# A matvec on VectorE: turning its result rows into columns through DRAM instead of on TensorE

## The chip, the cores and the metric

The kernel runs on one core of a Trainium2 chip. The metric is the device time of one execution in microseconds, from the start to the end of the program on that core. The kernel before was timed three times; the median is 1687.03 us (1686.95 to 1689.38). A separate execution was taken with the hardware profiler: it took 1689.57 us, and its span, from the first to the last instruction in the trace, is 1687.9 us.

The engines appear under short names: PE is TensorE (PEld its weight loads), DVE is VectorE, ACT is ScalarE, POOL is GpSimd, SP is SyncE, which in this kernel only issues transfers.

## The reference

One layer of a transformer-like backbone with token mixing and an MLP, for 128 context tokens and 256 latent tokens (384 in all), width 2048. Each of the two groups of tokens has a condition vector (c_ctx and c). From it the layer computes six modulation vectors of 2048 values:

```python
def _adaln(cond, ada_w, ada_b):
    mod = jax.nn.silu(cond) @ ada_w + ada_b          # (2048) @ (2048, 6*2048)
    return mod.reshape(cond.shape[0], N_MOD, D_MODEL)

# in the layer:
shift_a, scale_a, gate_a, shift_f, scale_f, gate_f = ...   # mod[:, 0..5]
h = _rmsnorm(x, norm_w[0]) * (1 + scale_a) + shift_a
...                                                  # projections, mLSTM heads, pooling
mix = jnp.concatenate([hm, hp], axis=-1) @ w_out
x = x + gate_a * _rmsnorm(mix, norm_w[1])
h = _rmsnorm(x, norm_w[2]) * (1 + scale_f) + shift_f
y = jnp.square(jax.nn.relu(h @ w1)) @ w2             # hidden width 8192
x = x + gate_f * _rmsnorm(y, norm_w[3])
```

Everything is float32. The change touches only how shift_f, scale_f and gate_f are brought into the layout in which they are used. What is computed stays the same.

## The kernel before

**Layout.** Activations are kept transposed: a tile holds 128 features (one per partition) by 384 tokens. A modulation value belongs to a feature, so it is needed as a column: one value per partition. The tile `mod` (line 212) is 128 x 6 x 16 x 2: for each of the six vectors (index i; 1 is scale_a, 2 gate_a, 3 shift_f, 4 scale_f, 5 gate_f), each of the 16 blocks of 128 features, and each of the two groups of tokens, one value per partition.

**Large products.** Each float32 product is made of three faster matmuls: both operands are split into a high and a low part. A weight piece of 512 KB is loaded by SP (`load_w`, line 122), ACT makes the high part (line 134), DVE the low part (line 135), and PE does high x high, high x low, low x high (lines 143 to 145). Three raw pieces and four high and low pieces (N_W) may be in flight. The order of the stages is: input projection (lines 481 to 520), then q and k with attention and pooling beside them, the output gate o, the output projection `w_out` (line 896; 32 pieces, for eight groups of 256 columns: four each, the first two groups in turns), then the MLP: w1 and w2. For chunks 1 to 7 of the MLP the w2 product is made in seven block products instead of eight (`mlp_seven`, lines 1192 to 1270; its matmuls are lines 1222 to 1224, its splits lines 1208 and 1209).

**The modulation vectors.** Some of them are computed on PE (`ada_mat`, `ada_gate`, `ada_eight`). The rest are made by `ada_vec(i, c, n)` (line 292) on DVE, as a generator which the large products advance step by step (`Feed`, line 150). It does a matvec for n columns of `ada_w` and both groups of tokens:

- The rows of `ada_w` are loaded in slabs, t = 0, 1, ... (line 300). For each slab and each group of tokens DVE multiplies by one value per partition and adds to the accumulator `ada_acc` (lines 314 and 316). With n = 1024 or in the later calls with n = 512 there are 16 slabs of one row per partition, two DVE operations each.
- Line 329: eight matmul records with a block of ones sum over the partitions. The sums appear in PSUM as rows: four rows (on partitions 0, 32, 64, 96), for two halves of the columns and two groups of tokens.
- Line 331: ACT copies them to `adav_sb` in SBUF. Then the generator yields.
- Line 335: matmuls with `adav_sb` as weights and four columns of the identity turn the rows into columns, in a fresh PSUM bank `adaf`: four matmuls for n = 1024, two for n = 512.
- `ada_finish` (line 277), once per half: DVE adds the bias (line 280) and, for scales and gates, multiplies by a norm weight (lines 285 and 288), and writes `mod`.

It is called eight times. `mid_vec` (line 786) makes five calls with n = 1024 beside q, k, o and `w_out`: i = 4 twice, i = 3 twice, then i = 2 once. In each, `mat` (line 816), a part of gate_a made on PE, advances at some steps. `gate_f` (line 966) makes three calls with n = 512 for i = 5 beside the MLP, the last two at a quarter of a step per product (RATE_GS); after the last call PE transposes the whole of gate_f to rows (line 976, `gfT`), which POOL writes to DRAM (`gf_dram`, line 978) for use at the end of the kernel (line 1132).

**Order.** In the first part PE, DVE and ACT follow the written order, then, up to line 520, PE alone. In most of the rest a planner orders the instructions of each engine when the program is built: it takes the instructions whose inputs it expects to be ready, those written earlier first. Each engine then works through its list strictly in order, and an instruction that waits holds up those behind it. Transfers issued by POOL stand in POOL's list, between its own operations: the power of line 200 for the norms of attention, the masks of line 682, and loads and stores of states.

Of the kernel before, what the change touches and what calls it, by code (L numbers as in the profile page):

```python
# [7 lines left out]
F32 = mybir.dt.float32  # L8
# [5 lines left out]
P = 128  # L14
# [29 lines left out]
def hymba_kernel(  # L44
# [6 lines left out]
    nc = tc.nc  # L51
    w_in, w_out, w1, w2, ada_w = w_in[0], w_out[0], w1[0], w2[0], ada_w[0]

    const = ctx.enter_context(tc.tile_pool(name="const", bufs=1))
# [5 lines left out]
    dram = ctx.enter_context(tc.tile_pool(name="dram", bufs=1, space=bass.MemoryType.DRAM))  # L60

    def slot(name, dt=F32):
        return slots.tile([P, 386], dt, tag="t", name=name)

    def bank(name):
        return psum.tile([P, 512], F32, tag="ps", name=name)
# [172 lines left out]
    def ada_mat(parts, tags=("ada",), raws=None):  # L239


        n, nk = len(parts), parts[0][2]
        w, nj = nk * P, 8 // nk
        ps = bank(f"ada_{parts[0][0]}_{parts[0][1]}")
        for b, (i, k0, _) in enumerate(parts):
            c0 = i * D + k0 * P
            for j0 in range(0, 16, nj):
                tag = tags[b % len(tags)]
                raw = raws.pop(0) if raws else None
                if raw is None:  # L250
                    raw = (wp if tag == "lo" else adap).tile([P, nj, w], F32, tag=tag, name=f"ada_raw_{i}_{k0}_{j0}", bufs=N_W if tag == "lo" else N_ADA)
                    nc.sync.dma_start(raw, aw[:, j0:j0 + nj, c0:c0 + w])
                for a in range(nj):
                    j = j0 + a
                    g = j % 4
                    nc.tensor.matmul(ps[32 * g:32 * g + 32, 0:w], cT[:, j, 6 - 2 * b:38 - 2 * b], raw[:, a, :],
                                     start=b == 0 and j < 4, stop=b == n - 1 and j >= 12)
                if b < n - 1 or j0 + nj < 16:
                    yield
        yield from ada_rows(parts, ps)  # L260
# [16 lines left out]
    def ada_finish(i, k0, nk, ps):  # L277

        v = mod[:, i, k0:k0 + nk, :]
        nc.vector.tensor_tensor(  # L280
            v, ps,
            abias[:, i, k0:k0 + nk].unsqueeze(2).to_broadcast([P, nk, 2]), op=ALU.add)
        if i in (1, 4):
            w = nw[:, i // 2, k0:k0 + nk].unsqueeze(2).to_broadcast([P, nk, 2])
            nc.vector.scalar_tensor_tensor(v, v, 1.0, w, op0=ALU.add, op1=ALU.mult)
        elif i in (2, 5):
            w = nw[:, 1 if i == 2 else 3, k0:k0 + nk].unsqueeze(2).to_broadcast([P, nk, 2])
            nc.vector.tensor_tensor(v, v, w, op=ALU.mult)

    vec = {}  # L290

    def ada_vec(i, c, n):


        acc = vec["acc"].tile([P, 2, n], F32, tag="adaacc", name=f"ada_acc_{i}_{c}", bufs=1)
        c0, nj = i * D + c, vec["slab"] // n

        def load(t):
            raw = vec["pool"].tile([P, nj, n], F32, tag="ada", name=f"ada_raw_{i}_{c}_{t}", bufs=vec["bufs"])
            nc.sync.dma_start(raw, aw[:, nj * t:nj * t + nj, c0:c0 + n])  # L300
            return raw

        beside = vec.get("beside", {})
        raw = load(0)
        yield
        for t in range(16 // nj):
            if t in beside:
                next(beside[t], None)
            ahead = load(t + 1) if t < 16 // nj - 1 else None
            for a in range(nj):  # L310
                for g in range(2):
                    cj = sg[:, g, nj * t + a:nj * t + a + 1]
                    if t == 0 and a == 0:
                        nc.vector.tensor_scalar(acc[:, g, :], raw[:, a, :], cj, None, op0=ALU.mult)
                    else:
                        nc.vector.scalar_tensor_tensor(acc[:, g, :], raw[:, a, :], cj, acc[:, g, :], op0=ALU.mult, op1=ALU.add)  # L316
            raw = ahead
            if ahead is not None:
                yield
        yield  # L320
        w = n // 2
        nk = w // P
        if "end" in beside:
            next(beside["end"], None)
        ps = bank(f"adav_{i}_{c}")
        for h in range(2):
            for g in range(2):
                r = 32 * (2 * h + g)
                nc.tensor.matmul(ps[r:r + 32, 0:w], ones[:, 0:32], acc[:, g, h * w:(h + 1) * w], start=True, stop=True)
        sb = vec["pool"].tile([P, 512], F32, tag="adasb", name=f"adav_sb_{i}_{c}", bufs=1)  # L330
        nc.scalar.activation(sb[:, 0:w], ps[:, 0:w], AF.Copy)
        yield
        pf = bank(f"adaf_{i}_{c}")
        for k in range(nk):
            nc.tensor.matmul(pf[:, 4 * k:4 + 4 * k], sb[:, k * P:(k + 1) * P], ident[:, 0:P:32], start=True, stop=True)
        for h in range(2):
            ada_finish(i, c // P + nk * h, nk, pf[:, 0:4 * nk].rearrange("p (k r) -> p k r", r=4)[:, :, 2 * h:2 * h + 2])
        yield
# [87 lines left out]
    h = []  # L426
# [25 lines left out]
    def load_chunk(s, ci, after=(), later=None):  # L452
        kind, c0, w = chunks[ci]
        ks = slice(ksteps[s][0], sum(ksteps[s]))
        if kind == "u":
            n, pieces = w, [(0, wv_in[:, ks, U0 + c0:U0 + c0 + w])]
        else:
            n, pieces = w * P, [(0, wv_in[:, ks, V0 + c0 * P:V0 + (c0 + w) * P])]
            if c0 == 6:
                pieces.append((n, wv_in[:, ks, 4 * M:4 * M + 32]))  # L460
                n += 32
        return load_w(pieces, f"{kind}_{c0}_{s}", ksteps[s][1] * n, after, later) + (n,)
# [18 lines left out]
    for s in range(NS):  # L481
        for ci, (kind, c0, w) in enumerate(chunks):
            k0, nk = ksteps[s]
            hi, lo, n = w_first if s == 0 and ci < 2 else load_chunk(s, ci, h_ins if s == 0 else ())
# [301 lines left out]
    def mid_vec():  # L786
        for i, q in ((4, 0), (4, 1), (3, 0), (3, 1), (2, 0)):
            yield from ada_vec(i, 1024 * q, 1024)
# [100 lines left out]
    for cols in ([0, 256], [512], [768], [1024], [1280], [1536], [1792]):  # L889
        if cols[0] in (768, 1024, 1280):  # L890
            for m in range(2):
                n = len(early)
                t = y[n // 2][:, 1024 * (n % 2):1024 * (n % 2) + 1024].rearrange("p (j c) -> p j c", c=256)
# [72 lines left out]
    def gate_f():  # L966
        yield from ada_mat([(5, 0, 2), (5, 2, 2)], raws=early)
        for q in (1, 2, 3):
            yield from ada_vec(5, 512 * q, 512)
            if q == 1:  # L970
                vec["half"] = True
                while vec["half"]:
                    yield
        ps = bank("gfT")
        t = slot("gfT")[0:32, 0:P]
        nc.tensor.transpose(ps[0:32, 0:P], mod[:, 5].rearrange("p k g -> p (k g)"), ident)
        nc.vector.tensor_copy(t, ps[0:32, 0:P])
        nc.gpsimd.dma_start(gf_dram, t)
        yield
# [3 lines left out]
    for k in range(KT):  # L983
        xr.append(slot(f"xTr{k}"))
        nc.gpsimd.dma_start(xr[k][:, 0:NTOK], xT_dram[:, k, :])
    gfg = gate_f()

    def fill():
# [400 lines left out]
```

## Time and profile before

| | |
|---|---|
| time, median of 3 runs | 1687.03 us |
| time of the profiled execution | 1689.57 us |
| its span, first to last instruction | 1687.9 us |
| PE busy | 1656.9 us (98%) |
| DVE busy | 1340.3 us (79%) |
| ACT busy | 752.4 us (45%) |
| POOL busy | 130.9 us (8%) |
| bytes moved, mean rate | 320.95 MB, 190 GB/s |
| mean granted clock of PE | 0.997 |

The profile is one execution, seen by the hardware profiler. A row of the timeline has the start and the duration in microseconds, the engine, the line, the operation, the tile written and the tiles read, the shapes and a count; in brackets stand the idle time of the engine just before, and what ended it. The table of windows gives for each stretch its length and the busy time of each engine with the number of instructions, then PE's granted clock (1.00 is full), the mean busy share of the 16 DMA engines and what they moved in GB/s. The chain of waits is followed back from the last instruction: its rows are start, duration, engine, tile and line. Matmuls are pipelined, so their durations overlap: what one costs is read from the starts of its neighbours.

### The profile page before, as it was taken

To read this page: it belongs to the slowest core of one execution; us is meant where nothing else is said; L and a number is where in the kernel's file an instruction comes from. 1 tells how busy PE (TensorE), PEld (TensorE's weight loads), DVE (VectorE), ACT (ScalarE), POOL (GpSimd) and SP (SyncE) were. 2 spreads that over 40 slices of the span, in tenths; PEclk is the share of its full clock that TensorE was granted. 3 is DMA by queue.
4 is the path that set the end of the run, shared out by engine and by line. 5 is a ranking of instruction groups with operands and counts; after the bars stand their busy time and mean duration, and the time that the engine had idled before them with its cause. 6 is when DMAs were issued, how large, how long until landed. Compare 5 with 4: busy or idle time off the path is not lost.

```text
span 1687.9 us, 27859 instructions
## 1 busy us (share of the span) xinstructions
PE 1656.9 (98%) x10965; PEld 1582.5 (94%) x10965; DVE 1340.3 (79%) x2009; ACT 752.4 (45%) x1225; POOL 130.9 (8%) x181
## 2 busy tenths in 40 slices
PE   6999999999999999999999999999999999999997
PEld 4888999999999989989999999999999999999996
DVE  3677769898999959997797688988588488588688
ACT  4332355555443345543444444444444444444443
POOL 0000002221000024430000000000000000000120
PEclk9999999999999999999999999999999999999999
DMA  9999857777789964754546245544344443433653
GB/s 319 316 296 298 277 160 256 238 250 223 237 270 309 311 203 129 217 153 126 173 152 194 88 138 173 158 150 140 110 150 127 124 138 114 149 122 112 187 183 134
DMA packets 258195, 320.95 MB, mean 190 GB/s; under 512 B 14752, under 2 KB 223248, under 8 KB 257680
## 3 DMA queue, kind: packets, MB, share of 16 engines
q1 hardware_dynamic: 250256, 303.41, 57.0%
q0 software_dynamic: 5856, 13.69, 2.8%
q10 hardware_dynamic: 1952, 2.07, 0.4%
q8 instruction: 86, 1.41, 0.3%
q14 instruction: 45, 0.37, 0.1%
HBM read 308.61 MB, written 10.51 MB: 189 GB/s over the span
## 4 chain that ended last, share of the span: by engine, by line
PE 90%; DVE 4%; DMA 3%; issue 1%; SPq 1%; ACT 0%; POOL 0%; DVEq 0%; ACTq 0%; POOLq 0%
PE acc_w L144 10%; PE acc_w L143 10%; PE acc_w L145 10%; PE y L1223 4%; PE y L1224 4%; PE y L1222 4%; PE v L495 4%; PE u L495 3%; PE acc_wo L143 3%; PE acc_wo L144 3%; PE acc_wo L145 3%; PE y_yz L1223 2%; PE y_yz L1222 2%; PE y_yz L1224 2%; PE y L1066 2%; PE y L1065 2%
## 5 line engine op out<-in xcount | busy, mean ns | idle before, releaser
L144 PE MATMUL acc_w<-h2l,hi_w 128*128 128x384 f32 (+1 forms) x1024 | 346.2, 338 | 0.5 <-DVE h2l L1016 0.5
L143 PE MATMUL acc_w<-h2h,hi_w 128*128 128x384 f32 (+1 forms) x1024 | 344.2, 338 | 1.2 <-ACT h2h L1012 1.2
L145 PE MATMUL acc_w<-h2h,lo_w 128*128 128x384 f32 (+1 forms) x1024 | 345.1, 337 | 0.0
L135 DVE TENSOR_TENSOR lo_w<-raw_w,hi_w 128x1024 fp32r<-128x1024 f32 x152 | 185.3, 1221 | 137.0 <-ACT hi_w L134 136.8
L134 ACT ACTIVATE hi_w<-raw_w 128x1024 fp32r<-128x1024 f32 x152 | 160.8, 1058 | 215.2 <-PE acc_w L144 94.9
L316 DVE SCALAR_TENSOR_TENSOR ada_acc<-ada_raw,sg,ada_acc 128x1024 f32<-128x1024 f32 (+1 forms) x240 | 252.0, 1080 | 0.8 <-DMA ada_raw<-in_ada_w_dram 0.7
L143 PEld LDWEIGHTS acc_w<-h2h,hi_w 128*128 128x128 f32 x1024 | 192.2, 188 | 2.8 <-ACT h2h L1012 2.0
L144 PEld LDWEIGHTS acc_w<-h2l,hi_w 128*128 128x128 f32 x1024 | 192.6, 188 | 1.2 <-DVE h2l L1016 0.8
L145 PEld LDWEIGHTS acc_w<-h2h,lo_w 128*128 128x128 f32 x1024 | 192.4, 188 | 0.3 <-DVE lo_w L135 0.2
L1208 ACT ACTIVATE hi_t<-w 128x1024 fp32r<-128x1024 f32 x104 | 109.6, 1060 | 119.1 <-DVE w L1244 34.3
L1209 DVE TENSOR_TENSOR lo_t<-w,hi_t 128x1024 fp32r<-128x1024 f32 x104 | 126.3, 1220 | 15.1 <-ACT hi_t L1208 14.8
L1209 DVE TENSOR_TENSOR lo_b<-w,hi_b 128x1024 fp32r<-128x1024 f32 x78 | 95.3, 1221 | 41.9 <-ACT hi_b L1208 41.6
L1208 ACT ACTIVATE hi_b<-w 128x1024 fp32r<-128x1024 f32 x78 | 82.5, 1059 | 98.1 <-PE acc_w L144 66.7
L134 ACT ACTIVATE hi_wo<-raw_wo 128x1024 fp32r<-128x1024 f32 x32 | 34.0, 1064 | 80.6 <-DMA raw_wo<-in_w_out_dram 57.4
L942 ACT ACTIVATE z<-acc_w 128x384 f32<-128x384 f32 x54 | 26.3, 487 | 75.1 <-PE acc_w L145 75.1
L495 PE MATMUL v<-hi_v,hh 128*128 128x384 f32 (+1 forms) x144 | 48.0, 333 | 0.0
L134 ACT ACTIVATE hi_v<-raw_v 128x768 fp32r<-128x768 f32 (+1 forms) x24 | 19.0, 793 | 64.4 <-DMA raw_v<-in_w_in_dram 55.6
L495 PE MATMUL v<-lo_v,hh 128*128 128x384 f32 (+1 forms) x144 | 46.6, 324 | 1.0 <-DVE lo_v L135 1.0
L495 PE MATMUL v<-hi_v,hl 128*128 128x384 f32 (+1 forms) x144 | 46.5, 323 | 0.0
L135 DVE TENSOR_TENSOR lo_wo<-raw_wo,hi_wo 128x1024 fp32r<-128x1024 f32 x32 | 38.8, 1217 | 7.8 <-ACT hi_wo L134 7.0
L143 PE MATMUL acc_k<-hh,hi_k 128*128 128x384 f32 x128 | 44.2, 345 | 0.0
L143 PE MATMUL acc_o<-hh,hi_o 128*128 128x384 f32 x128 | 43.9, 343 | 0.0
(2264 smaller groups left out, 4549.0 us busy)
## 6 DMA issues: line engine op xcount, KB each, us to landing
raw_w<-in_w_dram SPq DMA_DIRECT2D x152, 512.0 KB, 4.2
ada_raw<-in_ada_w_dram SPq DMA_DIRECT2D x130, 512.0 KB, 4.7
w<-in_w_dram SPq DMA_DIRECT2D x104, 512.0 KB, 4.1
raw_wo<-in_w_out_dram SPq DMA_DIRECT2D x32, 512.0 KB, 5.1
u<-in_ada_w_dram SPq DMA_DIRECT2D x18, 512.0 KB, 6.6
raw_u<-in_w_in_dram SPq DMA_DIRECT2D x16, 512.0 KB, 7.0
raw_q<-in_w_in_dram SPq DMA_DIRECT2D x16, 512.0 KB, 4.8
raw_k<-in_w_in_dram SPq DMA_DIRECT2D x16, 512.0 KB, 4.9
```

The costliest lines, as they stand in the source:

```text
L134: nc.scalar.activation(hi[:, 0:n], raw[:, 0:n], AF.Copy)
L135: low = lambda: nc.vector.tensor_tensor(lo[:, 0:n], raw[:, 0:n], hi[:, 0:n].bitcast(F32), op=ALU.subtract)
L143: nc.tensor.matmul(ps, lh, rh, start=start, stop=False)
L144: nc.tensor.matmul(ps, lh, rl, start=False, stop=False)
L145: mm3.ins = nc.tensor.matmul(ps, ll, rh, start=False, stop=stop).ins
L316: nc.vector.scalar_tensor_tensor(acc[:, g, :], raw[:, a, :], cj, acc[:, g, :], op0=ALU.mult, op1=ALU.add)
L495: nc.tensor.matmul(acc[i][:, 0:n], h[k0 + k][a][:, i * P:(i + 1) * P], (hi, lo)[b][:, k, :], start=k == 0 and a + b == 0, stop=k == nk - 1 ...
L1208: nc.scalar.activation(hi, raw, AF.Copy)
L1209: nc.vector.tensor_tensor(lo, raw, hi.bitcast(F32), op=ALU.subtract)
L1222: nc.tensor.matmul(acc, xh, wh, start=start and j == 0, stop=False)
L1223: nc.tensor.matmul(acc, xh, wl, start=False, stop=False)
L1224: nc.tensor.matmul(acc, xl, wh, start=False, stop=stop and j == 3)
```

## The change

In every call but that for i = 2, the matmuls of line 335 and the bank `adaf` are left out. Instead POOL issues three transfers. Two write the rows of `adav_sb` to a DRAM tile `rows`, a row of 128 values for each block of features and each group of tokens. The third reads it back transposed: partition p of `cols` receives element p of each row, so source and destination meet element by element (4 bytes). `cols` has one buffer. `ada_finish` is not called there, but put on the list `turned`, as one call for both halves. It is called in the next call of `ada_vec`, at t = 5; for the last call of gate_f, directly ahead of the transposition `gfT`.

```diff
-    vec = {}
+    vec, turned = {}, []
...
         for t in range(16 // nj):
+            if t == 5 and turned:
+                turned.pop()()
             if t in beside:
                 next(beside[t], None)
...
         nc.scalar.activation(sb[:, 0:w], ps[:, 0:w], AF.Copy)
         yield
+        if i != 2:
+            cols = const.tile([P, 8, 2], F32, tag="cols", name=f"adac_{i}_{c}", bufs=1)[:, 0:2 * nk]
+            rows = dram.tile([2 * n // P, P], F32, name=f"adar_{i}_{c}")
+            for h in range(2):
+                nc.gpsimd.dma_start(rows[2 * nk * h:2 * nk * h + 2 * nk].rearrange("(k g) p -> g k p", g=2),
+                                    sb[64 * h:64 * h + 64:32, 0:w].rearrange("g (k p) -> g k p", p=P))
+            with nc.allow_non_contiguous_dma(reason="rows to columns"):
+                nc.gpsimd.dma_start(cols.rearrange("p k g -> p (k g)"), rows.rearrange("r p -> p r"))
+            turned.append(lambda: ada_finish(i, c // P, 2 * nk, cols))
+            return
         pf = bank(f"adaf_{i}_{c}")
         for k in range(nk):
             nc.tensor.matmul(pf[:, 4 * k:4 + 4 * k], sb[:, k * P:(k + 1) * P], ident[:, 0:P:32], start=True, stop=True)
...
                 vec["half"] = True
                 while vec["half"]:
                     yield
+        turned.pop()()
         ps = bank("gfT")
         t = slot("gfT")[0:32, 0:P]
         nc.tensor.transpose(ps[0:32, 0:P], mod[:, 5].rearrange("p k g -> p (k g)"), ident)
```

## Prediction, made before the changed kernel was run

> **What bounds the kernel now.** I read the page first (busy shares, the chain that ended last), then the table of windows, then the chain piece by piece where it leaves PE, then the timeline around the lines that the change touches.
>
> ```profile
> span 1687.9 us, 27859 instructions
> PE 90%; DVE 4%; DMA 3%; issue 1%; SPq 1%; ACT 0%; POOL 0%; DVEq 0%; ACTq 0%; POOLq 0%
> core 0: us, PE busy (x) PEld busy (x) DVE busy (x) ACT busy (x) POOL busy (x), PEclk, DMA share, GB/s
> 470.00:600.00 130.00, 129.25 (x747) 126.14 (x749) 120.83 (x130) 47.40 (x74) 5.46 (x10) 0.99 0.90 297
> 650.00:850.00 200.00, 200.00 (x1106) 185.97 (x1105) 176.02 (x303) 94.38 (x157) 46.62 (x69) 1.00 0.55 164
> 1100.00:1290.00 190.00, 190.00 (x1383) 189.45 (x1383) 144.71 (x173) 86.17 (x104) 0.00 (x0) 1.00 0.42 131
> ```
>
> Nine tenths of the chain is PE, and in the stretches where the removed matmuls stand PE is never idle for more than 0.75 us. The granted clock is 0.99 to 1.00, so a matmul taken out there is time taken out, unless something else becomes late. Between these stretches the chain leaves PE once for long, from 858 to 911 us:
>
> ```profile
> 857.84 0.13 PE y_x L1224
> ...
> 857.99 0.39 ACT r L1265
> 858.39 1.21 DVE lo_w L135
> ```
>
> It enters that stretch from PE: a matmul of y_x ends, ACT copies, DVE splits. So what PE saves ahead of 858 us moves the whole stretch forward; that it does not is one of the rivals.
>
> **The change part by part.** *What it removes.* Seven of the eight calls of ada_vec lose the matmuls of line 335 and their bank.
>
> ```profile
> L335 PE MATMUL adaf<-cst,adav_sb x52: 167/252/273, 325.5 to 1286.4; 128*128 128x4 f32 x52
> 604.96 0.33 PE L145 MATMUL acc_wo<-mx15h,lo_wo 128*128 128x384 f32 x1
> 605.13 0.95 PE L335 MATMUL adaf<-cst,adav_sb 128*128 128x4 f32 x8
> 605.94 0.42 PE L143 MATMUL acc_wo<-mx0h,hi_wo 128*128 128x384 f32 x1
> 606.20 0.33 PE L144 MATMUL acc_wo<-mx0l,hi_wo 128*128 128x384 f32 x1
> ```
>
> There are 52 records because a matmul shows as two passes: five calls of 1024 columns make 4 matmuls, three of 512 make 2, so 26. What a group costs PE is read from starts, not durations, since they overlap. Matmuls of this stage start 0.17 us apart (604.96, 605.13). Without the eight records, line 143 would start at 605.13 and line 144 at 605.30; it starts at 606.20. A group of eight costs 0.90 us, one of four half, 0.45. Removed are four groups of eight (shift_f and scale_f; the one quoted, of gate_a, stays) and three of four (gate_f): 4 x 0.90 + 3 x 0.45 = 4.95 us. One group also waited:
>
> ```profile
> 541.99 0.60 ACT L331 ACTIVATE adav_sb<-adav 128x512 f32<-128x512 f32 x1 [0.49 <-PE ada_gate L272]
> 542.64 1.06 PE L335 MATMUL adaf<-cst,adav_sb 128*128 128x4 f32 x8 [0.75 <-ACT adav_sb L331]
> ```
>
> The next instruction of PE there is an acc_wo matmul that needs nothing from this copy, so the 0.75 us go too, and nothing else is late: **5.7 us** in all.
>
> On DVE two ada_finish per call become one: 24 small operations become 12.
>
> ```profile
> L280 DVE TENSOR_TENSOR mod<-adaf,prmT x16: 144/154/167, 326.5 to 1287.3; 128x8 f32<-128x8 f32 x10, 128x4 f32<-128x4 f32 x6
> ```
>
> At 0.15 us that is 1.8 us of DVE, beside PE: I count nothing.
>
> *What it adds.* Per call, on POOL: two transfers of rows to DRAM, then one of columns back, which waits until the rows have landed, and whose pieces are single elements of 4 bytes: 128 x 16 = 2048 (shift_f, scale_f) or 1024 (gate_f). No such transfer is in the trace. The nearest rows (name, KB, us to landing; then POOL's issue time in ns):
>
> ```profile
> x_dram<-x1b POOLq DMA_DIRECT2D x64, 48.0 KB, 3.5
> C<-in_state_C_dram POOLq DMA_DIRECT2D x8, 128.0 KB, 4.4
> out_dram<-mnew POOLq DMA_DIRECT2D x2, 0.0 KB, 2.0
> gf_dram<-gfT POOLq DMA_DIRECT2D x1, 16.0 KB, 3.7
> L1038 POOL DMA_DIRECT2D x_dram<-x1b x64 | 39.4, 622 | 45.5 <-DVE x1b L1035 36.9 <-DVE h2l L932 4.5 <-DVE h2n L927 3.2
> L660 POOL DMA_DIRECT2D C<-in_state_C_dram x8 | 5.9, 737 | 44.8 <-PE pool L533 29.2 <-DVE dn L740 5.9 <-PE inter L732 5.0
> ```
>
> Call T the time from the end of the copy (line 331) to the columns landed. Rows: two issues of 0.62 and a landing of 3.7 (2.0 at least, mnew). Issue of the columns: x_dram has 384 pieces of 128 bytes and takes 0.62, C 256 pieces and 0.74, so the count hardly shows: 0.62 below; above, in proportion, 8 x 0.74 = 5.9; I take 2.0. Landing: C's 4.4, plus the pieces. Spread over the 16 engines of the page, that is 128 per engine. x_dram has 24 per engine and lands no later than gf_dram with two, so a piece may cost nothing; against mnew it is (3.5 - 2.0)/24 = 62 ns; if the whole 3.5 us were pieces, 146 ns. I take 30, half of 62: 3.8 us. Then T = 1.2 + 3.7 + 2.0 + 4.4 + 3.8 = 15.1 us, between 1.2 + 2.0 + 0.6 + 4.4 = 8.2 and 1.2 + 3.7 + 5.9 + 4.4 + 18.7 = 33.9. For gate_f, with half the pieces: 1.2 + 3.7 + 1.2 + 4.4 + 1.9 = 12.4.
>
> A rule that speaks against the change: the Trainium skill, "DMA: Bandwidth & Descriptors", section "Rules for kernel authors", says that a last dimension that isn't contiguous becomes one descriptor per element and should be rearranged; its section "Bandwidth" gives about 10.5 ns per packet at small sizes. By that, if every element were a packet, 2048 elements are an estimated 21.5 us, T would be 32.8, and the sum a loss; no run here shows such a transfer yet.
>
> *What it moves.* ada_finish now stands at t = 5 of the next call. DVE works in order, so if the columns are late, it waits there, and lo_w, lo_wo and the splits behind it wait too, and then PE for them. One of the calls with ample room:
>
> ```profile
> 471.42 0.59 ACT L331 ACTIVATE adav_sb<-adav 128x512 f32<-128x512 f32 x1
> 489.85 1.27 DVE L316 SCALAR_TENSOR_TENSOR ada_acc<-ada_raw,sg,ada_acc 128x1024 f32<-128x1024 f32 x1
> ```
>
> The second is the 11th operation of the next call's accumulation (two per t), where t = 5 begins: 17.8 us after the copy. T = 15.1 fits. The last call of shift_f is tighter, since the next accumulation began before the copy at 541.99:
>
> ```profile
> 532.00:550.40 18.40, 11.19 (x10) 0.91 1.05 344
> 548.04 4.87 DVE L316 SCALAR_TENSOR_TENSOR ada_acc<-ada_raw,sg,ada_acc 128x1024 f32<-128x1024 f32 x4
> 552.82 1.22 DVE L135 TENSOR_TENSOR lo_wo<-raw_wo,hi_wo 128x1024 fp32r<-128x1024 f32 x1
> 400.00:553.00 153.00, 22.30 (x21) 0.99 0.83 266
> 561.97 0.34 PE L143 MATMUL acc_wo<-mx8h,hi_wo 128*128 128x384 f32 x1
> 562.33 0.34 PE L145 MATMUL acc_wo<-mx8h,lo_wo 128*128 128x384 f32 x1
> ```
>
> Ten operations (first row) are done by 550.4, so t = 5 begins there, 7.8 us after the copy ended at 542.59: DVE waits here for about 15.1 - 7.8 = 7.3 us. Behind it stand two accumulations (2.4) and lo_wo of 552.82 (1.2), which belongs to the 21st of 32 pieces of w_out (fourth row counts hi_wo on ACT); PE needs that one at 562.33 as the first of its sixth group of columns, and 1.65 earlier after the change, 560.7. With the addition itself (0.2), 560.7 - 542.6 - 3.8 = 14.3: up to T = 14.3 the lead of PE hides the wait, beyond it PE loses T - 14.3. At 15.1 that is **0.8 us**.
>
> The last call has no next one; finish and the transposition gfT follow at once.
>
> ```profile
> 1275.67 0.36 ACT L331 ACTIVATE adav_sb<-adav 128x256 f32<-128x256 f32 x1
> 1287.25 0.23 DVE L280 TENSOR_TENSOR mod<-adaf,prmT 128x4 f32<-128x4 f32 x2
> 1296.50 0.27 PE L976 MATMUL gfT<-cst,mod 128*32 128x128 f32 x1
> ```
>
> Columns at 1276.03 + 12.4 = 1288.4, finished at 1288.8. PE's turn for gfT lies between the place of the old matmuls (1286.2, in front of DVE's 1287.25) and its old place (1296.50): a loss of 2.6 to nothing. The planner puts an instruction where it expects it to be ready, so I take near the lower end, **0.5**.
>
> *POOL.* After the copies of shift_f and gate_f it is idle; beside attention the wait for the rows may hold up the power of line 200, for which DVE waits:
>
> ```profile
> 321.64 1.66 POOL L200 TENSOR_TENSOR rsh<-rsh,mhalf 128x2 f32<-128x2 f32 x1 [1.20 <-DVE rsh L199]
> 323.34 0.43 DVE L745 TENSOR_TENSOR hs<-hs,rsh 128x256 f32<-128x256 f32 x1 [0.60 <-POOL rsh L200]
> 579.83 0.58 POOL L985 DMA_DIRECT2D xTr<-xT_dram  x1 [105.74 <-DMA raw_wo<-in_w_out_dram]
> 1297.93 0.52 POOL L978 DMA_DIRECT2D gf_dram<-gfT  x1 [553.37 <-DVE gfT L977]
> ```
>
> That is at most a rows landing, 3.7 us. The lead that hides it is that of the splits, 562.33 - 554.04 = 8.3 us in the rows above; without it, 3.7 us at each of two calls. I count nothing. The same lead covers weights delayed by the pieces (3.8 us of 16 engines that are full there, share 1.05).
>
> **Sum.** 5.7 - 0.8 - 0.5 = 4.4 us less. The profiled execution took 1689.57 (span 1687.9 and 1.67 around it) and would take 1685.2; the median of before is 1687.03, 2.54 below it, so **1682.7**.
>
> **The rivals.** *The wait takes the place of the matmuls.* At 62 ns a piece (landing 4.4 + 7.9; issue 3.3, which is x_dram's 0.62 in proportion to its pieces) T is 1.2 + 3.7 + 3.3 + 12.3 = 20.5: PE loses 6.2 at 550 us and, with 1.2 + 3.7 + 1.7 + 4.4 + 4.0 = 15.0 for gate_f (finished at 1291.4), up to 5.2 at gfT. With 5.7 saved that is 1687.5 to 1692.7, the lower part likelier for the reason given above; T between 15.1 and 20.5 fills what lies between it and the forecast. For it: the DMA engines are full just there. Against: x_dram's landing shows no cost per piece.
>
> *Slower: one piece, one full cost.* The same wait at 550 us with the pieces near their upper bound. It decides from T = 14.3 + 5.7 = 20.0, and beyond 23.4 the loss exceeds 3.4 us. At 90 ns a piece and an issue of 3.3, T = 1.2 + 3.7 + 3.3 + 4.4 + 11.5 = 24.1 and the loss 9.8, so 1691.1; near 146 ns the other three calls lose too (from 17.8 + 8.3 = 26.1 on), and 33.9 gives 19.6 + 3 x 7.8 - 5.7 = 37 us more, 1724. The Trainium skill's rule cited above is this rival. Against it stands again x_dram.
>
> *The gain is not carried past 858 us.* If DVE's own backlog paced that stretch, the 4 x 0.90 + 0.75 + 0.45 = 4.8 us saved ahead of it would be lost, and 0.9 stay: 1686.1. The quoted chain speaks against it.
>
> **How the numbers follow.** Forecast 0.50 (its own range 1680.5 to 1683.6: no wait at all gives 1681.3, and a planner that orders anew may add 0.8); the wait in place 0.25; not carried 0.08; slower 0.17. About 0.2%, 3.4 us, is what a measurement of this kernel tells from no change. So faster 0.50, same 0.33, slower 0.17 (the upper end of the first rival counted with the slower). The range 1680.5 to 1690.5 leaves out that last case and a little below.
>
> **What would show it.** After: no adaf on PE but for eight records; three POOL transfers behind each copy, the third landing 8 to 14 us after its issue; DVE idle before mod (line 280) near 550 us with the columns' transfer as releaser, some 7 us, and PE idle under 2 us behind it; gfT on PE without a long wait; PE's busy time about 5 us less. The prediction is wrong if the third transfer takes over 20 us, if PE waits for lo_wo near 560 us or for mod at gfT by more than 3 us, or if the 858 us stretch begins no earlier than now.

## The result, and the profile after

The changed kernel is slower. Six runs of each, taken in turns on the same chip:

| | median, us | lowest to highest |
|---|---|---|
| before | 1687.83 | 1686.95 to 1689.73 |
| after | 1696.41 | 1694.31 to 1697.30 |

The ratio is 1.0046, 95% interval 1.0036 to 1.0056; of 1687.83 us that is 7.8 us more (6.1 to 9.5). It is an estimate from all the runs, not the quotient of the two medians, which lie 8.6 us apart; the same holds for the ratios below. The prediction was 1682.7, its range ended at 1690.5.

The page of after (span, busy time by engine, the queue of POOL's transfers) and the windows that were quoted of before:

```profile
span 1694.9 us, 27805 instructions
PE 1656.5 (98%) x10921; PEld 1580.3 (93%) x10921; DVE 1338.2 (79%) x1997; ACT 751.2 (44%) x1225; POOL 148.8 (9%) x202
...
q0 software_dynamic: 6592, 13.78, 3.0%
```

```profile
470.00:600.00 130.00, 126.59 (x721) 121.81 (x720) 113.59 (x124) 44.80 (x69) 5.21 (x7) 0.97 0.85 273
650.00:850.00 200.00, 198.88 (x1076) 184.34 (x1075) 177.80 (x313) 94.06 (x163) 50.50 (x74) 1.00 0.56 164
1100.00:1290.00 190.00, 190.00 (x1381) 189.34 (x1380) 142.68 (x174) 87.54 (x109) 2.57 (x4) 1.00 0.42 128
```

PE is as busy as before (1656.5 against 1656.9 us), although nearly 5 us of matmuls are gone: a busy PE at half clock counts as busy too. In the first window PE has become idle for 3.4 us (0.75 before), and its clock fell from 0.99 to 0.97; the second has 1.1 us of idle time, the third none. More shows where two matmuls that both kernels have are followed: the first sum of squares behind `w_out` (line 908 before, 920 after), and the first w2 matmul of the last chunk.

The timeline of PE, before and then after:

```profile
614.45 0.72 PE L908 MATMUL tr_r<-cst,sqa 128*128 128x1 f32 x6
...
1613.44 0.28 PE L1222 MATMUL y_x<-hi_b,hid56h 128*128 128x256 f32 x1
```

```profile
620.15 0.72 PE L920 MATMUL tr_r<-cst,sqa 128*128 128x1 f32 x6
...
1620.56 0.28 PE L1235 MATMUL y_x<-hi_b,hid56h 128*128 128x256 f32 x1
```

5.7 us are lost by the end of `w_out`, where some 4 should have been won, and 1.4 more in the MLP, where the matmuls of gate_f are gone as well.

**The transfers did nearly what was foreseen.** Groups of after by line (min/median/max in ns), and the issues (KB, median us to landing):

```profile
L342 POOL DMA_DIRECT2D adac<-adar x7: 917/1195/1218, 327.3 to 1273.8; - x7
...
adac<-adar POOLq DMA_DIRECT2D x4, 8.0 KB, 7.0
adac<-adar POOLq DMA_DIRECT2D x3, 4.0 KB, 4.9
```

The third transfer is issued in 1.2 us and lands 7.0 us after the issue began, a little sooner than the 8 to 14 us that the prediction gave. The queue's row of before (packets, MB, share of 16 engines) stands against the 6592 packets of after:

```profile
q0 software_dynamic: 5856, 13.69, 2.8%
```

That is 736 packets more for seven calls with 4 x 2048 + 3 x 1024 = 11,264 pieces of 4 bytes.

**The first place, 536 to 564 us.** The last call of shift_f in after, in the timeline of ACT, POOL, DVE and PE:

```profile
536.10 0.60 ACT L333 ACTIVATE adav_sb<-adav 128x512 f32<-128x512 f32 x1 [4.15 <-PE ada_gate L272]
...
536.99 1.15 POOL L339 DMA_DIRECT2D adar<-adav_sb  x2 [62.03 <-ACT adav_sb L333]
542.43 1.20 POOL L342 DMA_DIRECT2D adac<-adar  x1 [4.30 <-DMA adar<-adav_sb]
...
549.80 0.17 DVE L280 TENSOR_TENSOR mod<-adac,prmT 128x16 f32<-128x16 f32 x1 [7.20 <-DMA adac<-adar]
549.89 1.28 DVE L318 SCALAR_TENSOR_TENSOR ada_acc<-ada_raw,sg,ada_acc 128x1024 f32<-128x1024 f32 x1
...
550.07 0.30 ACT L1028 ACTIVATE h2h<-mod 128x2 fp32r<-128x2 f32 x2 [8.74 <-DVE mod L280]
...
551.09 0.55 DVE L885 TENSOR_TENSOR sqa<-sqa,sq_mo 128x384 f32<-128x384 f32 x1
551.56 1.28 DVE L318 SCALAR_TENSOR_TENSOR ada_acc<-ada_raw,sg,ada_acc 128x1024 f32<-128x1024 f32 x1
...
551.76 1.08 ACT L134 ACTIVATE hi_wo<-raw_wo 128x1024 fp32r<-128x1024 f32 x1
...
552.75 0.55 DVE L885 TENSOR_TENSOR sqa<-sqa,sq_mo 128x384 f32<-128x384 f32 x1
...
553.17 0.34 PE L144 MATMUL acc_wo<-mx0l,hi_wo 128*128 128x384 f32 x1
...
553.22 2.47 DVE L318 SCALAR_TENSOR_TENSOR ada_acc<-ada_raw,sg,ada_acc 128x1024 f32<-128x1024 f32 x2
...
555.62 1.22 DVE L135 TENSOR_TENSOR lo_wo<-raw_wo,hi_wo 128x1024 fp32r<-128x1024 f32 x1
...
556.89 0.69 PE L145 MATMUL acc_wo<-mx0h,lo_wo 128*128 128x384 f32 x1 [3.38 <-DVE lo_wo L135]
...
562.81 0.34 PE L145 MATMUL acc_wo<-mx3h,lo_wo 128*128 128x384 f32 x1
```

DVE waits 7.20 us for the columns (7.3 had been worked out). From 549.80 on it has no wait any more, but four accumulations and two sums of squares (`sqa`) stand in its list ahead of `lo_wo`, which ends at 556.84, 7.1 us after the columns landed. PE has run out of work by then and waits 3.38 us for it.

ACT waits as well, which was not worked out: the row of line 1028. ACT copies the finished shift_f into extra columns of the MLP's input, the planner has put these copies right behind the finish, and ACT, in its own order, waits 8.74 us for them. Behind them stand four evacuations and `hi_wo` (551.76). But this `hi_wo` is ready at 552.84, 2.8 us before DVE comes to `lo_wo`. So it is DVE's list, and not ACT's, that PE waits for here. Then PE's clock falls. The table of windows of after behind that wait:

```profile
556.00:558.00 2.00, 1.11 (x3) 1.11 (x4) 2.00 (x3) 0.00 (x0) 0.00 (x0) 0.50 0.98 341
558.00:560.00 2.00, 2.00 (x8) 2.00 (x8) 2.00 (x3) 0.00 (x0) 0.00 (x0) 0.50 1.09 376
560.00:562.00 2.00, 2.00 (x8) 2.00 (x7) 2.00 (x3) 1.06 (x1) 0.00 (x0) 0.50 1.05 343
562.00:564.00 2.00, 2.00 (x11) 2.00 (x10) 2.00 (x3) 0.00 (x0) 0.00 (x0) 0.80 0.95 298
```

The third number from the right is the granted clock: 0.50 for 6 us and 0.80 for 2, so 0.5 x 6 + 0.2 x 2 = 3.4 us of clock. In the first 0.9 us of it PE still waited, so the two may not simply be added. What the place costs is read from starts: from 553.17 to 562.81 us PE makes 19 steps, from a matmul of `mx0l` to one of `mx3h`, in 9.64 us; before makes the same 19 in 3.31 us (553.75 to 557.06). The place costs 6.3 us, 3.4 of them the wait and 2.9 the clock.

**The second place, 330 to 430 us, in attention.** The longest of PE's waits there, in after:

```profile
419.04 0.89 PE L744 MATMUL inter<-C,q 128*128 128x129 f32 x4 [2.14 <-DVE hs L754]
```

With three shorter ones (0.53, 0.29 and 0.49 us) and a clock of 0.86, 0.50 and 0.79 in the three windows of 2 us from 418 on, that is 3.45 + 1.7 = 5.1 us. No finish waits for columns here. The candidates were POOL, which holds up its masks while it waits for the rows (4.33 us at 395.72), and the order of the work.

### The profile page after: what moved, and what is told of

Its sections match the earlier page's. It is cut to its first block, busy times and chain, and to the rows that moved or that the text cites. A ratio compares the mean times of both kernels' runs of the same rounds, so it can differ in the third digit from the quotient of the medians.

```text
span 1694.9 us, 27805 instructions
## 1 busy us (share of the span) xinstructions
PE 1656.5 (98%) x10921; PEld 1580.3 (93%) x10921; DVE 1338.2 (79%) x1997; ACT 751.2 (44%) x1225; POOL 148.8 (9%) x202
## 3 DMA queue, kind: packets, MB, share of 16 engines
q0 software_dynamic: 6592, 13.78, 3.0%
## 4 chain that ended last, share of the span: by engine, by line
PE 55%; DVE 7%; DMA 3%; issue 2%; POOL 0%; ACT 0%; DVEq 0%; SPq 0%; ACTq 0%; POOLq 0%
PE acc_w L143 9%; PE acc_w L144 9%; PE acc_w L145 9%; PE y L1236 4%; PE y L1237 4%; PE y L1235 4%; PE y_yz L1236 2%; PE y_yz L1237 2%; PE y_yz L1235 2%; PE y L1079 2%; PE y L1077 2%; PE y L1078 2%; PE y_x L1235 1%; PE y_x L1236 1%; PE y_x L1237 1%
## 5 line engine op out<-in xcount | busy, mean ns | idle before, releaser
L339 POOL DMA_DIRECT2D adar<-adav_sb x14 | 8.6, 620 | 600.4 <-ACT adav_sb L333 600.4
```

## The experiments

All runs beside runs of the kernel before on the same chip; "us" is the ratio's distance from one, times the median of before beside it.

| run | what | median | before | ratio, 95% | us |
|---|---|---|---|---|---|
| e1 | matmuls out, no transfers | 1687.21 | 1687.96 | 0.9991 (0.9983 to 1.0000) | -1.5 |
| e2 | transfers beside the old way | 1689.44 | 1687.96 | 1.0007 (0.9998 to 1.0016) | +1.2 |
| e3 | finish at t = 12 | 1690.86 | 1687.96 | 1.0017 (1.0008 to 1.0026) | +2.9 |
| e4 | last shift_f by matmuls | 1690.45 | 1687.96 | 1.0019 (1.0010 to 1.0028) | +3.2 |
| e5 | change, step kept | 1692.07 | 1688.59 | 1.0027 (1.0015 to 1.0039) | +4.6 |
| e6 | step kept, finish at t = 12 | 1687.82 | 1688.59 | 0.9999 (0.9988 to 1.0010) | -0.2 |
| e7 | as e1, step kept | 1684.76 | 1688.59 | 0.9980 (0.9972 to 0.9989) | -3.4 |
| e8 | before, step left out | 1690.28 | 1688.59 | 1.0016 (1.0008 to 1.0025) | +2.7 |
| e9 | shift_f, scale_f only, as e6 | 1684.46 | 1688.27 | 0.9979 (0.9969 to 0.9988) | -3.5 |
| e10 | gate_f only, as e6 | 1692.03 | 1688.27 | 1.0027 (1.0018 to 1.0036) | +4.6 |

**e1, the matmuls taken out alone.**

```diff
...
-            turned.append(lambda: ada_finish(i, c // P, 2 * nk, cols))
+            turned.append(lambda: ada_finish(i, c // P, 2 * nk, abias[:, i, 0:2 * nk].unsqueeze(2).to_broadcast([P, 2 * nk, 2])))
             return
```

> Leaves out the turning of the rows for seven of the eight calls, so that shift_f, scale_f and gate_f lack their matvec: no matmuls of adaf, no transfers, and the finish (one per call, in the places of the change) adds the bias alone. Theory A (the removal is worth what was worked out, 5.7 us, and the waits that the transfers bring cost the rest): 1687.8 - 5.7 = 1682.1, or about 1680.4 if the half clock of 1.7 us that follows the old wait of 0.75 us at 542 us goes too. Theory B (the new order of the instructions costs by itself, whatever is waited for): 1687 or more.

Measured 1687.21, theory B's number. The planner put these additions, which wait for nothing, at 9 us, not in the places of the change; and still attention lost what it lost in after:

```profile
393.97 1.03 PE L675 MATMUL mb<-mrow,pick 104*128 104x384 f32 x4
...
419.90 0.71 PE L737 MATMUL inter<-C,q 128*128 128x129 f32 x4 [2.04 <-DVE hs L747]
```

So the second place needs neither a transfer nor a wait of POOL. It comes with the order.

**e2, the transfers alone.** The matmuls and both finishes stay, nobody reads the columns.

```diff
...
-            turned.append(lambda: ada_finish(i, c // P, 2 * nk, cols))
-            return
...
-        turned.pop()()
```

> Keeps the matmuls and both finishes of before and adds the three transfers of each of the seven calls, whose columns nobody reads. Theory A (pieces and weights delayed cost nothing, the finish's waits are what costs): within 1 us of before, 1687 to 1689. Theory C (POOL, which holds its issue of the columns until the rows have landed, delays the mask selects that DVE and then PE wait for at 390 to 420 us): 3 to 5 us more than before, 1691 to 1693, with PE idle near 419 us as after the change. Theory D (2048 pieces delay the weights near 550 us): PE waits for lo_wo near 557 us here too.

+1.2 us with an interval of -0.3 to 2.7: theory A. No wait for `hs` at 419 and none for `lo_wo` at 557 in its trace. The pieces, the traffic and POOL's waits cost little or nothing.

**e3, the finish later.**

```diff
-            if t == 5 and turned:
+            if t == 12 and turned:
```

> The change, but the finish stands at t = 12 of the next call instead of t = 5. Theory A (6.8 us are lost at 545 to 563 us because the finish stands where the columns have not landed: DVE waits 7.2 us, ACT's copies of shift_f behind it 8.7 us in order, hi_wo and lo_wo stand behind these): that loss goes, 1696.4 - 6.8 = 1689.6, with no wait over 1 us of PE between 545 and 563. The loss of about 5 us at 330 to 430 us stays. Theory D (the transfers themselves delay what PE needs there): 1695 or more.

1690.86. By the ratios that is 4.9 us less than after, where 6.8 had been expected, and between 545 and 563 us PE is never idle: the first place is the finish's place. The wait for `hs` at 421.91 us is still 2.15 us. DVE's and ACT's waits both go with this edit; that PE waited for DVE's is read from the rows of after above.

**e4, the last call of shift_f by matmuls.**

```diff
-        if i != 2:
+        if i != 2 and (i, c) != (3, 1024):
```

> The change for six calls; the last call of shift_f (the one of 542 us) keeps its matmuls and both finishes. Theory A: the 6.8 us at 545 to 563 us go, and 0.75 of wait, 1.7 of half clock behind it and 0.9 of matmuls come back: 1696.4 - 6.8 + 3.35 = 1693.0. Theory D (transfers of that call delay the weights): the same number, so this run tells where, not by what. If it gives less than 1691, more is lost behind this call than the 6.8 us.

1690.45, so under the 1691 named. The interval (+1.7 to +4.7 us) does not carry a conclusion from that half microsecond; the place is confirmed, more is not.

**The step that the change leaves out.** The diff moves one thing more. Before, `ada_vec` yields once after the copy to `adav_sb` and once more after its finishes. The changed code returns after the first. Each of the seven calls therefore takes one step fewer of the interleaving, and everything of the later calls stands earlier in the written order, from which the planner works. With a yield ahead of the return, PE's order up to the end of `w_out` is that of before but for the removed groups and a few small shifts. Four runs test it.

**e5 and e6, the change with the step.**

```diff
             turned.append(lambda: ada_finish(i, c // P, 2 * nk, cols))
+            yield
             return
```

> The change, with a yield ahead of its return, so that a call of ada_vec takes as many steps of the interleaving as before. Theory E (the return left out one step per call; every later call therefore stands earlier in the written order, the planner orders attention anew, hs is late for inter at 419 us, and the half clock follows): the 5 us at 330 to 430 us go, and the next accumulation starts a step later, so that the finish at t = 5 has more room and the 6.8 us at 545 to 563 us shrink too: 1687.8 - 5.7 + 0 to 2 = 1682 to 1684. Theory C (the transfers on POOL cost the 5 us in attention): 1690 or more. Theory A without E (only the place of the finish matters): 1695.

e6 has the same and `t == 12`.

> The change with that yield, and the finish at t = 12 instead of t = 5. Theory E and A together: no wait at 419 and none at 550 us, 1687.8 - 5.7 = 1682.1, or 1680.4 if the half clock behind the old wait of 0.75 us goes too. If it gives the same as the run with the yield alone, the wait at t = 5 was already covered there. Theory B (any new order costs): 1687 or more.

e5 came to 1692.07: the 5 us in attention are gone (PE is busy for all of 330 to 430 us, at a clock of 1.00), but the finish still waits, only later, and ACT with it. Here PE waits for ACT too: 0.85 us for a `hi_wo` that stands behind ACT's copies. Timeline of e5, DVE, ACT, PE:

```profile
566.81 0.18 DVE L280 TENSOR_TENSOR mod<-adac,prmT 128x16 f32<-128x16 f32 x1 [4.66 <-DMA adac<-adar]
...
567.08 0.39 ACT L1029 ACTIVATE h2h<-mod 128x2 fp32r<-128x2 f32 x3 [6.96 <-DVE mod L280]
...
569.98 0.45 PE L143 MATMUL acc_wo<-mx0h,hi_wo 128*128 128x384 f32 x1 [0.85 <-ACT hi_wo L134]
...
571.51 0.45 PE L145 MATMUL acc_wo<-mx0h,lo_wo 128*128 128x384 f32 x1 [0.91 <-DVE lo_wo L135]
```

The expectation that a step more would shrink this wait was half right (4.66 us instead of 7.20): the accumulation began a step later, but so did the copy. e6 has no wait there, and PE reaches the sums of squares 6.0 us ahead of before, as expected. But it ends at -0.2 us (-2.0 to 1.7): what was gained is lost behind 800 us.

**e7, the matmuls taken out alone, with the step.** As e1, with the yield.

> The run without turning once more (shift_f, scale_f and gate_f lack their matvec, no matmuls of adaf, no transfers), with the yield ahead of the return. Theory E: the order of PE is that of before less the matmuls, so the removal shows its worth: 1680.4 to 1682.1 instead of the 1687.2 without the yield. If it stays at 1687, the matmuls were worth nothing and the 5.7 us of the prediction are wrong by themselves.

-3.4 us (-4.7 to -1.9), against -1.5 without the step. Better than e1, less than expected.

**e8, the kernel before without the step.** Nothing else is changed.

```diff
             ada_finish(i, c // P + nk * h, nk, pf[:, 0:4 * nk].rearrange("p (k r) -> p k r", r=4)[:, :, 2 * h:2 * h + 2])
-        yield
+        if i == 2:
+            yield
```

> The kernel before, with nothing changed but that the last yield of ada_vec is left out for the same seven calls: matmuls and both finishes stay, no transfers. Theory E: it loses what the change loses at 330 to 430 us, about 5 us, so 1692 to 1693, with PE waiting for hs near 419 us. Any other theory: as before, 1687.8.

+2.7 us (1.4 to 4.2). The order is what moves. The timeline of PE, before and then e8:

```profile
390.38 1.17 PE L670 MATMUL mb<-mrow,pick 104*128 104x384 f32 x4
...
392.36 1.04 PE L329 MATMUL adav<-ada_acc,cst 128*32 128x512 f32 x8
```

```profile
387.07 1.04 PE L329 MATMUL adav<-ada_acc,cst 128*32 128x512 f32 x8
...
392.91 1.03 PE L671 MATMUL mb<-mrow,pick 104*128 104x384 f32 x4
...
417.79 0.49 PE L733 MATMUL inter<-C,q 128*128 128x129 f32 x2 [0.63 <-DVE C L716]
419.63 0.71 PE L733 MATMUL inter<-C,q 128*128 128x129 f32 x4 [0.87 <-DVE hs L743]
```

The matvec's sums (`adav`) have moved ahead of `mb`, the first matmul of the next pair of heads, which starts 2.5 us later (3.6 in e1). What follows from it is later too: DVE starts its products with the weights `e` at 404.41 us (400.66 in before) and the state `C` at 415.79 (411.24), while PE comes to `inter` at 416.77, only 0.5 us later than before. So `C` and `hs` are late for it. The waits of PE are shorter here than in after, and no half clock follows; the expected 5 us were too many. Four differences give the price of the step: e8 2.7; e7 against e1 1.9; after against e5 3.2; e3 against e6 3.1. Those between two runs are uncertain by 2 us or a little more either way; e8 stands directly beside before.

**e9 and e10, the two halves.** e9 turns only shift_f and scale_f through DRAM (`if i in (3, 4)`), e10 only gate_f (`if i == 5`); both with the yield and `t == 12`.

> By transfers only the four calls of shift_f and scale_f, with the yield and the finish at t = 12; the three calls of gate_f keep their matmuls and both finishes. PE's order is then that of before less four groups of matmuls. Theory F (what the run with yield and finish at t = 12 lost behind 800 us comes from gate_f: DVE waits 3.3 us for its columns at 804 us and 3.7 us at 1282 us, and the splits behind it are late for PE): PE keeps its 6 us of 614 us to the end but for a small idle, 1688 - 4 to 6 = 1682 to 1684, better than both kernels. Theory G (any gain ahead of 830 us is lost there in a wait for something else): within 1 us of 1688.

> The other half: shift_f and scale_f keep their matmuls and finishes, the three calls of gate_f go by transfers, with the yield. Up to 614 us as before. Theory F: 1.35 us of matmuls saved, DVE's waits at 804 and 1282 us cost PE 1 to 4 us: 1688 to 1691. Theory G: 1686.5, the matmuls saved and nothing lost.

e9 is faster than both kernels: -3.5 us (-5.2 to -2.0). Its PE timeline, to be held against the two at the top:

```profile
608.26 0.72 PE L921 MATMUL tr_r<-cst,sqa 128*128 128x1 f32 x6
...
1607.03 0.28 PE L1235 MATMUL y_x<-hi_b,hid56h 128*128 128x256 f32 x1
```

6.2 us ahead of before at 614, 6.4 at 1613: what is won ahead of 858 us is carried to the end. (The profiled execution of before had a half clock that others lack, see below; by the ratio of all runs it is 3.5.)

e10 costs 4.6 us (3.0 to 6.1), more than theory F's upper end of 1691. Its timeline, the finishes of the first and the third call on DVE, then PE:

```profile
809.54 0.17 DVE L280 TENSOR_TENSOR mod<-adac,prmT 128x8 f32<-128x8 f32 x1 [3.48 <-DMA adac<-adar]
...
1284.55 0.17 DVE L280 TENSOR_TENSOR mod<-adac,prmT 128x8 f32<-128x8 f32 x1 [4.27 <-DMA adac<-adar]
```

```profile
835.23 0.39 PE L1236 MATMUL y_x<-hi_b,hid14h 128*128 128x256 f32 x1 [0.87 <-ACT hid14h L193]
...
899.07 0.39 PE L1237 MATMUL y_yz<-lo_b,hid9h 128*128 128x256 f32 x1 [1.99 <-DVE lo_b L1223]
...
1286.11 0.39 PE L1237 MATMUL y<-lo_t,hid33h 128*128 128x256 f32 x1 [0.82 <-DVE lo_t L1223]
```

The first finish is written at t = 12 of the next call, yet the planner has put it right behind the transfer, ahead of the next accumulation. DVE stands still at 809 and 1284 us, where its splits have little lead, and PE waits three times, 3.7 us in all. In e2, which makes the same transfers and keeps the matmuls, PE waits only once there, 0.31 us at 898.79. How much of the 4.6 us is the wait itself and how much the accumulations that now stand elsewhere was not tried apart; in e7, where DVE waits for no columns, PE still waits 0.88 us for `hid14h`, and against e9 nothing of gate_f's 1.35 us is seen.

So the 7.8 us of after can be walked, one edit at a time: shift_f and scale_f turned and well placed -3.5 (e9), gate_f with them +3.3 (e6 against e9), the finish at t = 5 instead of 12 +4.8 (e5 against e6), the step left out +3.2 (after against e5). Each step is uncertain by 2 us or a little more either way.

## Why the prediction was wrong

- **What is removed, 5.7 us:** right in kind, somewhat large. The four groups of shift_f and scale_f with the old wait were put at 4 x 0.90 + 0.75 = 4.35; e9 measures 3.5 (2.0 to 5.2), with the transfers in it. The 1.35 us of gate_f did not show in any run.
- **The length of the transfers, T = 15.1 and 12.4:** right in kind, 2 us too long. The copy ended at 536.70; the columns landed at 542.43 + 7.34 = 549.77 (the chain of waits has the landing as 7.34, from the start of the issue), so T is 13.1; for gate_f 10.1 (copy ended 1268.5, finish 1278.7). The sum had added 2.0 us of issue to the landing, which already holds it. The value of 30 ns for a piece was enough, and "one piece, one full cost" fell: the Trainium skill, "DMA: Bandwidth & Descriptors", section "Rules for kernel authors", would make a descriptor of each element; an estimate by that page was 21.5 us, and this trace shows 7.0 us and 736 packets for all seven calls. (The trace counts packets, not descriptors, so it is the price of a packet for each element that fell.)
- **The wait of DVE, 7.3 us, measured 7.20:** luck. T was 2.0 us shorter, and DVE stood at the finish 5.9 us after the copy (542.60, where the `lo_wo` ahead of it ended), not 7.8.
- **"Up to T = 14.3 the lead of PE hides it":** this is the step that failed first. It took the order of before: the finish at 550.4, two accumulations and `lo_wo` behind it (3.8 us with the addition), and PE in need of that `lo_wo` at 560.7. In after the finish stood at 542.6, ahead of a `lo_wo` that PE needed at 553.3, and 7.1 us of DVE's work lay between the landing and the end of that `lo_wo`. By the same formula the limit is 553.3 - 536.7 - 7.1 = 9.5, not 14.3; T of 13.1 lies 3.6 beyond it, and PE waited 3.38. (That was one of the signs named for being wrong: a wait for `lo_wo` near 560 us of more than 3 us.) The step kept does not rescue it: in e5 T is 13.9 and PE waits 0.85 and 0.91 us. e3 and e6, in which the columns are there in time, lose nothing at this place. The working also left out who reads `mod`. Here are the copies of shift_f in before, without a wait, in ACT's timeline:

```profile
546.77 0.47 ACT L1015 ACTIVATE h2h<-mod 128x2 fp32r<-128x2 f32 x4
```

  In after and e5 they follow the finish, and they stand in ACT's list ahead of the splits' high parts, so a wait on DVE became one on ACT too. In after it ended too early to matter, in e5 it is behind the 0.85 us.
- **The half clock:** no term of the sum had it. It nearly doubled the price of the wait (2.9 us behind 3.38 us), and added 1.7 in attention.
- **"A planner that orders anew may add 0.8":** the size was wrong, and the reason was not seen. The diff itself leaves out a step of the interleaving in seven calls; that costs 1.9 to 3.2 us by the four differences, and the traces show it in attention, a stretch of which the working only had POOL in view.
- **POOL, "I count nothing":** held. POOL waited 4.3 us for the rows, and e2 shows +1.2 us, with zero inside its interval.
- **gfT, "a loss of 2.6 to nothing":** the place was right, the mechanism not. PE does not wait for gfT. The finish waits ahead of it on DVE (3.5 to 5.5 us by run), and the first call's finish, which was taken to have ample room, waits 3.3 to 3.5 us near 809 because it was placed by the planner's view of the transfer and not where it is written. By e10 gate_f turned this way loses 4.6 us where the sum had a gain of 0.85.
- **The gain carried past 858 us:** right (e9).

The rival that ended slower had the direction with another cause: the pieces do not cost, the waits do. Where the working went wrong is that it worked out the waits in the order of before, and followed the change in the code only where it adds and removes instructions.

## What to carry to other kernels

When an operand's producer is moved behind a transfer, list what is queued between it and the next thing that the busiest engine needs, in the order of the new kernel and not of the old one, and list all readers of what it writes, on every engine: they wait with it. In a kernel that is interleaved by generators, count the yields of the old and the new path: a `return` in place of a last `yield` moves everything behind it. And put the finish where the transfer has landed with room to spare, or leave out the calls for which there is no such place: four of the seven calls, with the step kept and the finish at t = 12, made this change a gain of 0.21% (0.12 to 0.31%).

## What had not been expected of the hardware

**Short waits of PE can be followed by half clock, and need not be.** Windows of before behind the wait of 0.75 us at 542.64, and of e2 behind the same wait at 542.53:

```profile
543.00:545.00 2.00, 2.00 (x14) 2.00 (x14) 2.00 (x8) 0.35 (x1) 0.00 (x0) 0.89 1.09 375
545.00:547.00 2.00, 2.00 (x7) 2.00 (x7) 1.91 (x5) 1.20 (x4) 0.00 (x0) 0.50 1.04 367
547.00:549.00 2.00, 2.00 (x10) 2.00 (x10) 2.00 (x2) 0.23 (x3) 0.00 (x0) 0.76 1.11 349
```

```profile
545.00:547.00 2.00, 2.00 (x13) 2.00 (x12) 2.00 (x6) 0.96 (x1) 0.00 (x0) 1.00 1.05 362
```

Before lost 0.22 + 1.0 + 0.48 = 1.7 us of clock behind 0.75 us of waiting; e2 lost none. (From 540.95 to 543.56 PE had only matmuls of four columns besides this wait, so the wait alone need not be the cause; that was not tried.) In e6 two waits (1.42 us at 829.75, 0.87 at 831.37) were followed by a clock of 0.50 from 832 to 834 us. The 1.99 us in e10 at 899 were not, nor were 2.60 us in after at 906: the clock stayed at 1.00. In the twelve profiles, each fall of the clock ahead of the last matmuls took 1.7 us of clock or 3.4. The Trainium skill, "TensorE: Matmul & The Clock Gate", section "What's actually happening", has a window of some 3.4 us that runs freely and a clock of one half after an idle window. The length agrees with before: 1.7 us lost at a clock of one half are 3.4 us at it; and a free-running window would explain why one wait is followed by it and its like is not. Its section "Why this matters for your kernels" warns of idle gaps over about 3 us; here half clock followed a wait of 0.75 us and did not follow one of 2.60, so the length of a gap alone does not tell. For a sum this means that a wait of PE may cost itself alone or itself and 1.7 to 3.4 us more, and that single executions of one kernel can differ by that: the profile of e5 has two falls of 1.7 us, at 138 us and at 838 us, and took 1696.26 us, 4.2 more than its median.

**Transfers of 4-byte pieces were cheap:** 2048 of them were issued in 1.2 us and landed in 7.0, 1024 in 0.92 and 4.9; from DRAM that is 2.1 us for 1024 pieces more, 2 ns apiece. No run sends more than 2048 at once.
